# Two-layer MLA / sparse-attention / PEER trunk on one core: layer 1 reordered (indexer blocks first, selection between value blocks, attention two heads at a time inside the key projection, TensorE's order written out), and four query blocks of each PEER loaded early

## The chip, the core and the metric

One core of a Trainium2 chip runs the whole program. The metric is the device time of one execution in microseconds (us). The engines are named as in the profile: PE (matrix multiplication), PEld (PE's weight loads), DVE (vector engine), ACT (scalar engine), POOL (GpSimd), SP (the queue that issues the loads). They run side by side, each through its own list of instructions in order, and wait for each other through semaphores.

## What is computed

256 frames of 1024 channels go through two layers, in fp32 accuracy. Cut to what matters here:

```
layer 0: x = LayerNorm(alpha*x + MLA(x));   x = LayerNorm(alpha*x + PEER(x))
layer 1: x = LayerNorm(alpha*x + DSA(x));   x = LayerNorm(alpha*x + PEER(x))

DSA:  q, k, v (8 heads of 128), q_idx (8 heads of 64), k_idx (64), w_idx (8) = x @ w_in
      q, k, q_idx, k_idx = rope(...)
      idx_score = sum_h w_idx[h] * relu(q_idx[h] . k_idx), masked to chunks of 64 frames
      sel = top_k(idx_score, 64)          # the keys that a frame may look at
      out = softmax(q . k[sel] * 128**-0.5) . v[sel];   out @ w_o
PEER: q = x @ w_q (16 half-queries of 128);  s = q . sub_keys (16 times 128 scores)
      the 16 best expert pairs per head -> gate;  sum over experts of gate * gelu(x . down) * up
```

## The kernel before

**Operands.** Every large product is done in three passes over split operands: a weight block `raw` (128x1024 fp32, 512 KB) is loaded by SP into a ring of 4, ACT copies its high part `hi` (L83, `CAST`), and `lo = raw - hi` is made by DVE (L85), or by POOL for every third block while `ws.share` is 3. The rings of `hi` and `lo` hold 4 blocks each. `Stream.get` hands out block i and queues the `hi` and `lo` of block i+3 and the load of block i+6, so a `CAST` of block i+4 can start only when PE is done with block i. The input, transposed, is held as `xh`, `xl`. `proj` (L221) multiplies one block into a head's 128x256 tile (24 matmuls); `rows` (L238) multiplies the rows of the input by a block 512 columns at a time (12 matmuls for both halves of the frames). All matmuls are issued through `mm` (L213).

**PSUM.** There are 8 banks: four in a ring (`ps`), and four with fixed names (`py(0)` to `py(3)`).

**Layer 1's DSA** (`dsa`, L642). The order of the weight blocks is set by `ws.add`: eight value blocks, four indexer-query blocks (`qi`), the indexer-key block (`ki`, with the 8 columns of w_idx), eight query blocks `q`, eight key blocks (tiles also named `q`), eight blocks of the output projection. The first four value blocks are multiplied while layer 0 still ends. `heads` (L703) does two heads of queries or keys and then `rope`: two partition-swapping copies on ACT (L444, L445), one product on DVE (L448), one on POOL (L449), a sum on DVE (L452). Between the query heads stand `weigh` (L682: w_idx transposed on PE into `wi`) and `select` (L688: 8 small matmuls `il`, relu on ACT, weighted sums on DVE at L696, then 8 rounds of max and replace on DVE, L699 and L700, and the selection mask at L701), for each half of the frames.

**Attention** (`attention`, L454). `scores(h)` makes two score tiles (128 and 256 keys wide): matmul `s`, mask and row maximum on DVE (L470), a small product for the bias (L472), exponential on ACT (L473), reciprocal and scaling on DVE (L475). `output(h)` transposes the probabilities on PE into `pt` (L482 to L484), copies them back on ACT (L486), and multiplies by v into `o`, which is split into `xh`, `xl`. In layer 1 the last two key heads stand between `scores(1)` and the rest; the tile scheduler decides how the remaining PE instructions interleave. Both layers use this function. After it `out_proj` (L500) runs four heads of the output projection, and `finish` (L325) the last four with the residual sum and the LayerNorm, and, as `lead`, the first four query blocks of PEER, multiplied in rows into `qw`.

**PEER** (`peer`, L723). It begins by copying the two `qw` tiles to SBUF (L747), transposing them on PE (`qwT`, L750) and copying them back (L751). Then come the scores against the sub-keys (`ps`) for these four half-queries, the other twelve half-queries (`pq`, `proj` on two blocks each) with their scores in turn, and the search for experts (`choose`, L774, almost all DVE), which runs beside the `down` products (`d`) that follow.

Of the kernel before, what the change touches and what calls it, by code (L numbers as in the profile page):

```python
# [18 lines left out]
P = 128  # L19
# [24 lines left out]
FIRST = 4  # L44
GSCALE = 2.0 ** 14
# [5 lines left out]
class Stream:  # L51
# [5 lines left out]
    def __init__(self, nc, raw, hi, lo):  # L57
        self.nc, self.raw, self.hi, self.lo = nc, raw, hi, lo
        self.blocks, self.ready = [], []
        self.n_loaded = self.n_split = self.n_taken = 0  # L60
        self.tiles = []
        self.share = 0
# [4 lines left out]
    def _load(self, upto):  # L67
        while self.n_loaded <= min(upto, len(self.blocks) - 1):
            src, w = self.blocks[self.n_loaded]
            t = self.raw.tile([P, D], F32, tag="raw", name=f"raw{self.n_loaded}")  # L70
            self.last = self.nc.sync.dma_start(t[:, :w], src).ins
            self.tiles.append(t)
            self.n_loaded += 1

# [72 lines left out]
def tile_trunk(ctx: ExitStack, tc: tile.TileContext, ins, out: bass.AP):  # L147
# [55 lines left out]
    ws.add(ins["dsa_v"])  # L203
    ws.add(ins["dsa_iq"])
    ws.add(ins["dsa_ik"], 576)
    ws.add(ins["dsa_qk"])
# [4 lines left out]

    def mm(o, l, r, start, stop):
        return nc.tensor.matmul(o, l, r, start=start, stop=stop, skip_group_check=True)  # L213

    def mm3(o, lpair, rpair, start, stop):
# [3 lines left out]
        mm(o, ll, rh, False, stop)  # L219

    def proj(o, blk, w=P):  # L221

        h, l = blk
        for c in range(NC):
            s = slice(c * w, (c + 1) * w)
            mm3(o, (h[:, s], l[:, s]), (xh[:, c, :], xl[:, c, :]), c == 0, c == NC - 1)
# [227 lines left out]
    def attention(qk, v, mask, scale, oh, ol, ar, meanwhile):  # L454

        sring = ar.ring(6, T)
# [3 lines left out]
        def scores(h):  # L460
            pr = []
            for t in range(2):
# [3 lines left out]
                for i, (qT, kT) in enumerate(pairs):  # L466
# [12 lines left out]
        def output(h):  # L479
            pr = probs.pop(h)  # L480
            p = py(h % 2, f"pt{h}")
            nc.tensor.transpose(p[:, 0:128], pr[0], ident)  # L482
            nc.tensor.transpose(p[:, 128:256], pr[1][:, 0:128], ident)
            nc.tensor.transpose(p[:, 256:384], pr[1][:, 128:256], ident)  # L484
            pt = tring()
            nc.scalar.copy(pt, p[:, 0:384])  # L486
            o = py(2 + h % 2, f"o{h}")
# [3 lines left out]

        scores(0)
        scores(1)
        meanwhile()
        for h in range(HEADS):
            if 0 < h < HEADS - 1:
                scores(h + 1)
            output(h)
# [505 lines left out]
```

## Time and profile before

| what | value |
|---|---|
| median of 3 runs | 1878.99 us (1876.62 to 1880.26) |
| the profiled execution: its time | 1878.64 us |
| its span in the trace | 1876.7 us |
| granted PE clock, mean over the span | 0.998 |
| PE busy | 1840.9 us, 98% |
| DVE / ACT / POOL busy | 1326.3 us, 71% / 1052.4 us, 56% / 577.9 us, 31% |
| instructions | 33300, of which 12482 matmuls |

The span is what lies between the first and the last instruction in the trace; the execution's time is 1.9 us longer, and the median 0.35 us above that. A matmul's end is modelled: in a row of back-to-back 128x256 matmuls each is shown as 0.28 us long while the next starts 0.12 us after it, so idle time after a matmul is shown 0.16 us too short. DSA lies at about 930 to 1051 us of the span, the start of the two PEERs at 108 and 1062 us.

### The profile page before, as it was taken

What the parts mean: (1) busy time and instruction counts of PE and PEld (TensorE: products, weight loads), DVE (VectorE), ACT (ScalarE), POOL (GpSimd) and SP (SyncE); (2) the same over time, 40 slices, a digit from 0 to 9 for tenths busy, and PEclk for the clock granted to TensorE, in tenths of its full rate; (3) what the DMA queues carried; (4) which work ended last, traced back from release to release, by engine and by line L of the source; (5) the groups of instructions that cost most, each with busy time, mean ns of one, the idle gap of its engine ahead of it and who ended that gap; (6) DMA issues with size and microseconds to landing.
All of it is one profiled execution on the core that took longest, in us unless ns stands there. A gap on an engine that the chain in (4) does not pass through costs nothing. (4 is left out here: it accounts for less than half of the span.)

```text
span 1876.7 us, 33300 instructions
## 1 busy us (share of the span) xinstructions
PE 1840.9 (98%) x12482; PEld 1655.3 (88%) x12482; DVE 1326.3 (71%) x2764; ACT 1052.4 (56%) x1827; POOL 577.9 (31%) x650
## 2 busy tenths in 40 slices
PE   8999999999999999999998999999999999999998
PEld 7889999999998888888797799999999988888886
DVE  5679985788875555555678789957788765555555
ACT  6655455777764444444466445547777654444443
POOL 2001542999930000000032005509999700000000
PEclk9999999999999999999999999999999999999999
DMA  6455555444456555555654555564444465555553
GB/s 227 153 194 179 180 191 172 155 158 158 158 175 228 184 188 191 188 185 189 211 168 148 191 163 180 176 206 155 158 158 152 165 229 186 190 189 185 187 190 113
DMA packets 93762, 335.51 MB, mean 179 GB/s; under 512 B 10400, under 2 KB 11424, under 8 KB 93600
## 3 DMA queue, kind: packets, MB, share of 16 engines
q1 hardware_dynamic: 93312, 332.87, 52.9%
q8 instruction: 97, 1.59, 0.3%
q14 instruction: 65, 0.53, 0.1%
q10 hardware_dynamic: 288, 0.52, 0.1%
HBM read 329.16 MB, written 4.19 MB: 178 GB/s over the span
## 5 line engine op out<-in xcount | busy, mean ns | idle before, releaser
L85 DVE TENSOR_TENSOR lo<-raw,hi 128x1024 fp32r<-128x1024 f32 x587 | 725.6, 1238 | 365.7 <-ACT hi L83 364.6
L83 ACT CAST hi<-raw 128x1024 fp32r<-128x1024 f32 x592 | 618.8, 1046 | 591.7 <-PE d L213 259.5
L213 PE MATMUL d<-xh,hi 128*128 128x256 f32 x2048 | 579.4, 283 | 0.0
L213 PE MATMUL d<-xh,lo 128*128 128x256 f32 x2048 | 572.8, 280 | 0.9 <-DVE lo L85 0.9
L213 PE MATMUL d<-xl,hi 128*128 128x256 f32 x2048 | 572.9, 280 | 0.0
L847 POOL TENSOR_SCALAR VU<-iota,i2t 128x128 f16<-128x128 f16 x512 | 430.8, 859 | 112.1 <-DVE i2t L836 100.5
L213 PEld LDWEIGHTS d<-xh,lo 128*128 128x128 f32 x2048 | 384.5, 188 | 1.3 <-DVE lo L85 1.3
L213 PEld LDWEIGHTS d<-xh,hi 128*128 128x128 f32 x2048 | 384.7, 188 | 0.0
L213 PEld LDWEIGHTS d<-xl,hi 128*128 128x128 f32 x2048 | 384.1, 188 | 0.0
L213 PE MATMUL y<-lo,xh 128*128 128x512 f32 x1088 | 345.4, 394 | 0.0
L213 PE MATMUL y<-hi,xh 128*128 128x512 f32 x1088 | 345.0, 394 | 0.0
L213 PE MATMUL y<-hi,xl 128*128 128x512 f32 x1088 | 344.7, 394 | 0.0
L293 POOL TENSOR_TENSOR st<-st,mhalf 128x1 f32<-128x1 f32 x8 | 4.4, 554 | 855.2 <-DVE st L291 855.2
L213 PEld LDWEIGHTS y<-hi,xl 128*128 128x128 f32 x1088 | 203.5, 187 | 50.4
L213 PEld LDWEIGHTS y<-lo,xh 128*128 128x128 f32 x1088 | 203.4, 187 | 50.5 <-DVE lo L85 0.6
L213 PEld LDWEIGHTS y<-hi,xh 128*128 128x128 f32 x1088 | 203.4, 187 | 49.9
L848 DVE TENSOR_SCALAR VU<-iota,i1t,gt 128x128 f16<-128x128 f16 x512 | 139.2, 349 | 58.4 <-PE G L213 33.3
L849 ACT ACTIVATE U<-VU,gr 128x128 f16<-128x128 f16 x512 | 170.1, 399 | 1.2 <-DVE gr L832 0.7
L903 ACT CAST xh<-arena 128x512 fp32r<-128x512 f32 x128 | 79.4, 621 | 154.5 <-PE y L213 149.2
L904 DVE TENSOR_TENSOR xl<-arena,xh 128x512 fp32r<-128x512 f32 x128 | 88.1, 691 | 82.0 <-ACT xh L903 82.0
L802 POOL TENSOR_TENSOR arena<-arena 128x800 f32<-128x800 f16 x32 | 79.0, 2488 | 41.0 <-DVE arena L800 40.1
L213 PE MATMUL G<-VU 128*128 128x128 f16 x512 | 71.4, 221 | 6.9 <-DVE VU L848 4.1
(224 smaller groups left out, 1819.8 us busy)
## 6 DMA issues: line engine op xcount, KB each, us to landing
raw<-in_down SPq DMA_DIRECT2D x256, 512.0 KB, 3.3
raw<-in_up SPq DMA_DIRECT2D x256, 512.0 KB, 4.2
raw<-in_peer_q SPq DMA_DIRECT2D x32, 512.0 KB, 4.6
raw<-in_dsa_qk SPq DMA_DIRECT2D x16, 512.0 KB, 3.3
raw<-in_mla_w_o SPq DMA_DIRECT2D x8, 512.0 KB, 5.2
raw<-in_dsa_v SPq DMA_DIRECT2D x8, 512.0 KB, 3.5
raw<-in_dsa_w_o SPq DMA_DIRECT2D x8, 512.0 KB, 4.5
raw<-in_mla_qk SPq DMA_DIRECT2D x7, 512.0 KB, 4.7
```

The source lines that it names most:

```text
L83: nc.scalar.copy(hi, raw)
L85: eng.tensor_tensor(lo, raw, hi.bitcast(F32), op=ALU.subtract)
L213: return nc.tensor.matmul(o, l, r, start=start, stop=stop, skip_group_check=True)
L293: nc.gpsimd.tensor_tensor(st[:, 5:6], st[:, 4:5], mhalf, op=ALU.pow)
L802: nc.gpsimd.tensor_tensor(o.rearrange("p k c -> p c k"), same, cell[t][:, h, :, None].to_broadcast([P, CELLS, TOPK]), op=ALU.mult)
L847: nc.gpsimd.tensor_scalar(V, iota16, i2t[:, t : t + 1], None, op0=ALU.is_equal)
L848: nc.vector.tensor_scalar(U, iota16, i1t[:, t : t + 1], gt[:, t : t + 1], op0=ALU.is_equal, op1=ALU.mult)
L849: nc.scalar.mul(L, U, gr[:, t : t + 1])
L903: nc.scalar.copy(hh, a)
L904: nc.vector.tensor_tensor(al, a, hh.bitcast(F32), op=ALU.subtract)
```

## The change

Six things are done in one edit.

1. *Blocks of layer 1.* Order now: value blocks 0 to 3, `qi`, `ki`, value blocks 4 to 7, queries, keys, output projection. `weigh` stands behind value block 4; `select` became a generator, and `pick(n)` issues the next n of its `il` steps after each half of value blocks 5 to 7 and in the query projection.
2. *TensorE's order.* From value block 4 to the end of attention every PE instruction is tied behind the one emitted before it (`pe`, `chained`), so PE's list is the order of the code.
3. *Attention of layer 1.* Heads are done in pairs inside the key projection: scores of 0, 1 after two key pairs, and so on; heads 4 to 7 alternate with the first four heads of the output projection (`project`), and their `pt` and `o` use the ring `ps`. In layer 0 the scores run two heads ahead of the output. In both layers the product at L472 is dropped: the reduction scales, takes the minimum of the negated scores, and the exponential has scale -1.
4. *`lo` on POOL* only during the query projection, not during the key projection.
5. *PEER's start, both layers.* The transposes of `qw` are placed behind the first of the two blocks of `pq4`; then the scores of the first four half-queries, and the rest.
6. *Early loads, both layers.* When the output projection starts, PEER's query blocks 4 to 7 are loaded into a free part of the arena instead of into the ring `raw`. The loads of the residual `x` and of the LayerNorm's gain and bias are issued before the key projection.

```
+    def ahead(self, behind, places):
+        for i, t in enumerate(places, self.n_taken + behind):
+            assert i >= self.n_loaded and self.blocks[i][1] == D
+            self.last = self.nc.sync.dma_start(t, self.blocks[i][0]).ins
+            self.early[i] = t
...
-    ws.add(ins["dsa_v"])
+    ws.add(ins["dsa_v"][0:FIRST])
     ws.add(ins["dsa_iq"])
     ws.add(ins["dsa_ik"], 576)
+    ws.add(ins["dsa_v"][FIRST:NC])
     ws.add(ins["dsa_qk"])
...
+    def pe(emit):
+        with ExitStack() as order:
+            if chain["on"] and chain["last"] is not None:
+                order.enter_context(tc.issue_after(chain["last"]))
+            ins = emit()
+        chain["last"] = ins.ins
+        return ins
...
-        sring = ar.ring(6, T)
+        sring = ar.ring(2 * ahead + 2, T)
...
-                nc.vector.tensor_tensor_reduce(out=s, in0=p[:, :nk], in1=mask[t], scale=1.0, scalar=GONE,
-                                               op0=ALU.add, op1=ALU.max, accum_out=m[:, 0:1])
-                nc.vector.tensor_scalar(m[:, 1:2], m[:, 0:1], scale[t], -1.0, op0=ALU.mult, op1=ALU.mult)
-                nc.scalar.activation(s, s, AF.Exp, bias=m[:, 1:2], scale=scale[t], accum_out=m[:, 2:3])
+                nc.vector.tensor_tensor_reduce(out=s, in0=p[:, :nk], in1=mask[t], scale=scale[t], scalar=-GONE,
+                                               op0=ALU.add, op1=ALU.min, accum_out=m[:, 0:1])
+                nc.scalar.activation(s, s, AF.Exp, bias=m[:, 0:1], scale=-1.0, accum_out=m[:, 2:3])
...
+            p = ps(f"pt{h}") if late and h >= 4 else py(h % 2, f"pt{h}")
...
+            o = ps(f"o{h}") if late and h >= 4 else py(2 + h % 2, f"o{h}")
...
+        meanwhile(2)
+        pair(scores, 0)
+        meanwhile(4)
+        pair(scores, 2)
+        pair(turned, 0)
+        meanwhile(6)
+        pair(output, 0)
+        pair(turned, 2)
+        pair(scores, 4)
+        pair(output, 2)
+        pair(scores, 6)
+        for h in range(4, 8, 2):
+            late(h - 4, 0)
+            pair(turned, h)
+            late(h - 4, 1)
+            pair(output, h)
+            late(h - 3, 0)
+            late(h - 3, 1)
+
+    def project(oh, ol, h, t):
+        if h == t == 0:
+            with tc.issue_after(ws.last):
+                ws.ahead(HEADS + FIRST, [arena[:, EARLY + i * D : EARLY + (i + 1) * D] for i in range(4)])
+            begun["y4"] = [[py(2 * i + n, f"y{i}{n}") for n in range(2)] for i in range(2)]
+        if t == 0:
+            begun["w"] = ws.get()
+        rows(begun["y4"], (oh[:, h, :], ol[:, h, :]), begun["w"], h == 0, False, (t,))
...
+        chained(True)
+        v4 = begun.pop("v4")
+        for c in range(FIRST, NC):
+            for t in range(2):
+                rows(v4, (xh[:, c, :], xl[:, c, :]), blk := ws.get() if t == 0 else blk, False, c == NC - 1, (t,))
+                if c > FIRST:
+                    pick(2)
+            if c == FIRST:
+                weigh()
+                pick(1)
...
         ws.share = DSA_POOL
         for h in range(0, HEADS, 2):
-            heads(qT, h)
-            (weigh, lambda: select(0), lambda: select(1), lambda: None)[h // 2]()
-        for h in range(0, HEADS - 2, 2):
-            heads(kT, h)
+            heads(qT, h, lambda: pick(2))
+            pick(3)
+        pick(9)
+        ws.share = 0
...
+        queries(4)
+        scores(0)
+        queries(6)
+        scores(1)
+        for g4 in range(2, 4):
+            queries(4 * g4)
+            queries(4 * g4 + 2)
+            scores(g4)
```

The lists of the engines show three places at which instructions stand otherwise. In them a number behind `hi`, `q`, `o` or `pq` tells one tile from the next. The rows begin with the line of the kernel that issues the instruction: L95, L475, L476, L742, L743, L747, L748, L97, L479, L483, L260, L261, L518, L845 and L852 of the changed kernel are L83, L444, L445, L675, L676, L680, L681, L85, L448, L452, L229, L230, L486, L747 and L751 of the one before.

**First place: behind the indexer's key.** ACT's list of before, from the copies of `ki`:

```order
L83 CAST hi_10438<-raw_10336 128x1024
L675 COPY arena<-ki 32x256
L676 COPY arena<-ki 32x256
L83 CAST hi_10468<-raw_10366 128x1024
L681 ACTIVATE arena<-ki 8x256
L680 COPY arena<-arena 64x256
```

and of the changed kernel:

```order
L95 CAST hi_10341<-raw_10240 128x1024
L742 COPY arena<-ki 32x256
L743 COPY arena<-ki 32x256
L95 CAST hi_10363<-raw_10270 128x1024
L748 ACTIVATE arena<-ki 8x256
L747 COPY arena<-arena 64x256
```

In both a `CAST` stands ahead of the `ACTIVATE` that makes w_idx. Before, the next reader, `wi` on PE, comes 56 matmuls of the projections later. In the changed kernel `hi_10363` is in the ring the successor of `hi_10236`, which is value block 4, and PE's list has `wi` directly behind the last matmul of that block:

```order
L240 MATMUL v_10073<-lo_10237,xh 128x512
L240 MATMUL v_10072<-hi_10236,xl 128x512
L240 MATMUL v_10073<-hi_10236,xl 128x512
L243 MATMUL wi<-ident,arena 128x8 x2
L240 MATMUL v_10070<-hi_10266,xh 128x512
```

The `il` that follow are between the value blocks now; before, PE met `wi` inside the query projection.

**Second place: the end of the key projection.** PE's list of before, where `q6` is the tile of key heads 6 and 7, `sht` the scores of head h and half t, `pt` the transposed probabilities and `o` the output:

```order
L213 MATMUL q6_11037<-xl_91,hi323_10936 128x256
L213 MATMUL q6_11037<-xh_90,lo323_10937 128x256
L213 MATMUL s20_11113<-arena_98 128x128
L213 MATMUL s21_11121<-arena_98 128x256
L482 MATMUL pt0_11103<-ident_84,arena_98 128x128
...
L213 MATMUL s41_11173<-arena_98 128x256
L213 MATMUL s50_11191<-arena_98 128x128
L213 MATMUL o0_11108<-arena_98 128x256
L213 MATMUL o0_11108<-arena_98 128x128
L213 MATMUL s51_11199<-arena_98 128x256
L213 MATMUL o1_11134<-arena_98 128x256
```

and of the changed kernel:

```order
L240 MATMUL q6_11051<-xl_91,hi323_10948 128x256
L240 MATMUL q6_11051<-xh_90,lo323_10949 128x256
L240 MATMUL o0_11117<-arena_98 128x256
L240 MATMUL o0_11117<-arena_98 128x128
L240 MATMUL o1_11122<-arena_98 128x256
L240 MATMUL o1_11122<-arena_98 128x128
L243 MATMUL pt2_11127<-ident_84,arena_98 128x128 x3
```

Scores and transposes stood behind `q6`; now the outputs of heads 0 and 1 stand there. `o1` uses `py(3)`, the bank of `q6`. ACT's list of the changed kernel at this place:

```order
L95 CAST hi326_11082<-raw326_10952 128x1024
L95 CAST hi327_11211<-raw327_10982 128x1024
L475 COPY arena_98<-q6_11051 64x512
L476 COPY arena_98<-q6_11051 64x512
L260 CAST xh_90<-o0_11117 128x256
L260 CAST xh_90<-o1_11122 128x256
L518 COPY arena_98<-pt2_11127 128x384
```

and DVE's:

```order
L97 TENSOR_TENSOR lo326_11083<-raw326_10952,hi326_11082 128x1024
L97 TENSOR_TENSOR lo327_11212<-raw327_10982,hi327_11211 128x1024
L479 TENSOR_TENSOR arena_98<-q6_11051,arena_98 128x512
L261 TENSOR_TENSOR xl_91<-o0_11117,xh_90 128x256
L483 TENSOR_TENSOR arena_98<-arena_98 128x512
```

`hi327` is in the ring the successor of `hi323`, the block that the last matmul of `q6` reads. It stands ahead of the two copies that read `q6`, and its `lo327` ahead of the product that reads `q6`.

**Third place: the start of PEER in layer 1.** PE's and ACT's lists of before:

```order
L213 MATMUL qw1_11460<-lo335_11450,xh_90 128x512 x2
L213 MATMUL qw1_11460<-hi335_11449,xl_91 128x512 x2
L750 MATMUL qwT0_11537<-ident_84,arena_98 128x128 x4
L750 MATMUL qwT1_11544<-ident_84,arena_98 128x128 x4
L213 MATMUL pq10_11562<-xh_90,hi336_11563 128x256
```

```order
L83 CAST hi336_11563<-raw336_11498 128x1024
L747 COPY arena_98<-qw0_11459 128x512
L83 CAST hi337_11567<-raw337_11501 128x1024
L747 COPY arena_98<-qw1_11460 128x512
L751 COPY arena_98<-qwT0_11537 128x4x128
L83 CAST hi338_11571<-raw338_11517 128x1024
L751 COPY arena_98<-qwT1_11544 128x4x128
```

and of the changed kernel:

```order
L240 MATMUL pq4_11498<-xl_91,hi336_11499 128x256
L240 MATMUL pq4_11498<-xh_90,lo336_11500 128x256
L851 MATMUL qwT0_11545<-ident_84,arena_98 128x128 x4
L851 MATMUL qwT1_11551<-ident_84,arena_98 128x128 x4
L240 MATMUL pq4_11498<-xh_90,hi337_11503 128x256
```

```order
L845 COPY arena_98<-qw0_11427 128x512
L845 COPY arena_98<-qw1_11428 128x512
L95 CAST hi339_11511<-arena_98 128x1024
L95 CAST hi340_11557<-raw340_11515 128x1024
L852 COPY arena_98<-qwT0_11545 128x4x128
L852 COPY arena_98<-qwT1_11551 128x4x128
```

The transposes moved behind the 24 matmuls of the first block of `pq4`; the two copies of `qw` are no longer parted by a `CAST` of a block that comes through the ring `raw`.

## Rows read from the trace of the kernel before

**Rows 1.** The page: the span, the busy time of each engine, and the line of PE's granted clock in 40 equal slices, and the group of all `lo` on DVE (idle time behind the busy time and the mean).

```profile
span 1876.7 us, 33300 instructions
...
PE 1840.9 (98%) x12482; PEld 1655.3 (88%) x12482; DVE 1326.3 (71%) x2764; ACT 1052.4 (56%) x1827; POOL 577.9 (31%) x650
...
PEclk9999999999999999999999999999999999999999
...
L85 DVE TENSOR_TENSOR lo<-raw,hi 128x1024 fp32r<-128x1024 f32 x587 | 725.6, 1238 | 365.7 <-ACT hi L83 364.6
```

**Rows 2.** What PE waited for over the whole span: its tile and line, the releaser, us in total, times, longest.

```profile
PE qwT L750 <- ACT arena L747: 4.0, 4, 1.6
PE s L213 <- DVE arena L452: 2.8, 1, 2.8
...
PE s L213 <- DVE m L470: 1.0, 2, 0.7
...
PE d L213 <- DVE lo L85: 0.9, 2, 0.6
```

**Rows 3.** Three stretches of layer 1: us, then for each engine its busy time and instructions, PE's granted clock, the share of the DMA engines and GB/s.

```profile
930.40:1003.00 72.60, 69.78 (x540) 65.25 (x538) 55.23 (x95) 44.19 (x68) 24.79 (x13) 1.00 0.49 165
1003.00:1007.00 4.00, 4.00 (x17) 3.69 (x18) 3.96 (x10) 2.44 (x3) 1.77 (x1) 0.57 0.63 200
...
1012.00:1028.00 16.00, 13.56 (x77) 10.52 (x76) 14.21 (x74) 13.12 (x42) 2.16 (x1) 1.00 0.43 159
```

**Rows 4.** PE in order of time at the first scores: start, us, the instruction, and in brackets the idle time before it with its releaser.

```profile
999.87 0.28 PE L213 MATMUL q<-xh,lo 128*128 128x256 f32 x1
1002.98 2.45 PE L213 MATMUL s<-arena 128*128 128x128 f32 x8 [2.83 <-DVE arena L452]
```

**Rows 5.** DVE in order of time, at three places of the query and key projections.

```profile
960.14 2.51 DVE L679 TENSOR_TENSOR arena<-arena 64x256 f32<-64x256 f32 x1
...
998.60 3.39 DVE L85 TENSOR_TENSOR lo<-raw,hi 128x1024 fp32r<-128x1024 f32 x1
...
1002.25 0.67 DVE L452 TENSOR_TENSOR arena<-arena 128x512 f32<-128x512 f32 x1
...
1007.25 0.29 DVE L701 TENSOR_SCALAR arena<-arena 128x256 f32<-128x256 f32 x1
```

**Rows 6.** POOL in order of time at the same places.

```profile
959.74 2.63 POOL L85 TENSOR_TENSOR lo<-raw,hi 128x1024 fp32r<-128x1024 f32 x1 [1.98 <-ACT hi L83]
...
998.53 2.38 POOL L85 TENSOR_TENSOR lo<-raw,hi 128x1024 fp32r<-128x1024 f32 x1 [0.24 <-ACT hi L83]
...
1014.63 2.16 POOL L449 TENSOR_TENSOR arena<-arena 128x512 f32<-128x512 f32 x1 [8.59 <-ACT arena L445]
```

**Rows 7.** PE in order of time in the attention behind the key projection: the five instructions that waited.

```profile
1014.05 1.23 PE L213 MATMUL s<-arena 128*128 128x128 f32 x4 [0.27 <-DVE m L470]
1015.99 0.49 PE L213 MATMUL s<-arena 128*128 128x128 f32 x2 [0.71 <-DVE m L470]
...
1020.04 0.30 PE L482 MATMUL pt<-ident,arena 128*128 128x128 f32 x1 [0.36 <-DVE arena L475]
...
1023.49 0.92 PE L213 MATMUL o<-arena 128*128 128x256 f32 x4 [0.19 <-ACT arena L486]
...
1025.78 0.92 PE L213 MATMUL o<-arena 128*128 128x256 f32 x4 [0.76 <-ACT arena L486]
```

**Rows 8.** PE in order of time at the transposes of `qw`, layer 0 and layer 1.

```profile
112.82 0.66 PE L750 MATMUL qwT<-ident,arena 128*128 128x128 f32 x4 [1.60 <-ACT arena L747]
114.25 0.66 PE L750 MATMUL qwT<-ident,arena 128*128 128x128 f32 x4 [0.78 <-ACT arena L747]
...
1065.83 0.66 PE L750 MATMUL qwT<-ident,arena 128*128 128x128 f32 x4 [0.57 <-ACT arena L747]
1067.52 0.66 PE L750 MATMUL qwT<-ident,arena 128*128 128x128 f32 x4 [1.03 <-ACT arena L747]
```

**Rows 9.** ACT in order of time, behind the indexer's key and at the start of PEER in layer 1.

```profile
958.62 1.05 ACT L83 CAST hi<-raw 128x1024 fp32r<-128x1024 f32 x1 [0.38 <-PE q L213]
959.81 0.37 ACT L681 ACTIVATE arena<-ki 8x256 f32<-8x256 f32 x1
...
1064.24 1.05 ACT L83 CAST hi<-raw 128x1024 fp32r<-128x1024 f32 x1 [6.28 <-DMA raw<-in_peer_q]
1065.20 0.58 ACT L747 COPY arena<-qw 128x512 f32<-128x512 f32 x1
1065.93 1.05 ACT L83 CAST hi<-raw 128x1024 fp32r<-128x1024 f32 x1 [0.16 <-DMA raw<-in_peer_q]
```

**Rows 10.** PE in order of time around a group of `il`.

```profile
967.20 0.28 PE L213 MATMUL q<-xl,hi 128*128 128x256 f32 x1
967.32 0.28 PE L213 MATMUL q<-xh,lo 128*128 128x256 f32 x1
967.52 0.72 PE L213 MATMUL il<-arena 64*128 64x128 f32 x8
968.17 0.39 PE L213 MATMUL q<-xh,hi 128*128 128x256 f32 x1
```

**Rows 11.** The experts' search in both layers: first stretches as in rows 3 (the queries and the beginning of the search, then the rest of it, for each layer).

```profile
118.60:158.90 40.30, 40.30 (x348) 40.30 (x347) 33.47 (x145) 18.95 (x25) 0.00 (x0) 1.00 0.54 177
158.90:264.20 105.30, 104.73 (x891) 104.53 (x889) 105.12 (x367) 54.51 (x63) 49.87 (x48) 1.00 0.52 173
```

More of the change, by code (lines that the diff above doesn't have):

```diff
@@ L44 @@
 FIRST = 4
+EARLY = 11264
 GSCALE = 2.0 ** 14
@@ L61, in __init__ @@
         self.tiles = []
+        self.early = {}
         self.share = 0
@@ L452, in rope, with attention @@
             nc.vector.tensor_tensor(place, t1[r], xs[r], op=ALU.add)
-    def attention(qk, v, mask, scale, oh, ol, ar, meanwhile):
-        sring = ar.ring(6, T)
+    def attention(qk, v, mask, scale, oh, ol, ar, ahead, meanwhile, late=None):
+        sring = ar.ring(2 * ahead + 2, T)
         tring = ar.ring(2, 384)
@@ L490, in output, with pair, out_proj @@
             split_ps(oh[:, h, :], ol[:, h, :], o[:, 0:256])
[L492 to L498, printed above, removed]
-    def out_proj(oh, ol, g, b, x, spare):
-        y4 = [[py(2 * t + n, f"y{t}{n}") for n in range(2)] for t in range(2)]
-        for h in range(HEADS - STAGGER):
-            rows(y4, (oh[:, h, :], ol[:, h, :]), ws.get(), h == 0, False)
+        if not late:
+            for h in range(HEADS + ahead):
+                if h < HEADS:
+                    meanwhile(h)
+                    scores(h)
+                if h >= ahead:
+                    turned(h - ahead)
+                    output(h - ahead)
+            return
+        def pair(f, h):
+            f(h)
+            f(h + 1)
+        meanwhile(2)
[24 more added lines that the diff above has]
+        rows(begun["y4"], (oh[:, h, :], ol[:, h, :]), begun["w"], h == 0, False, (t,))
+    def out_proj(oh, ol, g, b, x, spare, start):
+        for h in range(start, HEADS - STAGGER):
+            for t in range(2):
+                project(oh, ol, h, t)
+        y4 = begun.pop("y4")
         finish(y4, lambda h: (oh[:, h, :], ol[:, h, :]), HEADS, g, b, x, spare, lead_queries)
@@ L637, in qk @@
             return [(qn[:, h, :], kn[:, h, :]), (qr[:, h // 2, h % 2, :], kr)]
-        attention(qk, v, mask, [rq[:, t : t + 1] for t in range(2)], oh, ol, ar, values)
-        out_proj(oh, ol, g, b, x, r2)
+        attention(qk, v, mask, [rq[:, t : t + 1] for t in range(2)], oh, ol, ar, 2,
+                  lambda h: values() if h == 2 else None)
+        out_proj(oh, ol, g, b, x, r2, 0)
     def dsa():
@@ L658, in dsa @@
         m8 = ar.take(2, 8)
-        v4 = begun.pop("v4")
-        for c in range(FIRST, NC):
-            rows(v4, (xh[:, c, :], xl[:, c, :]), ws.get(), False, c == NC - 1)
-        for t in range(2):
-            for n in range(2):
-                nc.scalar.copy(v[:, t, n * 512 : (n + 1) * 512], v4[t][n])
         for h in range(0, HEADS // 2, 2):
@@ L690, in select @@
             for h in range(HEADS):
+                yield
                 r = slice((h % 2) * 64, (h % 2) * 64 + 64)
@@ L701, in select, with heads @@
             nc.vector.tensor_scalar(sel[t], acc[t], GONE / 2, NEG, op0=ALU.is_gt, op1=ALU.mult)
-        def heads(dst, h):
+        def heads(dst, h, between=lambda: None):
             p = py(h // 2, f"q{h}")
```

88 lines of the change are left out of this document (60 added, 28 removed).

## The prediction

> **What bounds the kernel now.** I read the page first: PE is busy 1840.9 of 1876.7 us and its granted clock shows no tenth below 9 in any slice [rows 1]. So TensorE is the bound; the change alters neither number nor kind of its matmuls, and can gain only what PE stands idle or runs at the lower clock, 36 us in all. The list of what PE waits for is next: the largest waits that the diff touches are the transposes of `qw` behind their copies on ACT (4.0 us, 4 times), one wait of the first scores for a rope sum on DVE (2.8), and small ones in attention [rows 2]. Then I cut layer 1 into stretches. [...]
>
> Why the first scores waited is read on DVE and POOL. PE's last key matmul starts at 999.87, the scores at 1002.98 [rows 4]; they need the sum at L452, which DVE begins at 1002.25, because a `lo` ahead of it took 3.39 us [rows 5], while POOL made another `lo` from 998.53 for 2.38 us [rows 6]. All 587 `lo` on DVE take 1.24 us on average [rows 1]. The same picture stands at 960.14: a DVE sum of 64x256 takes 2.51 us [rows 5], and its neighbour of the same shape 0.41, while POOL's `lo` runs from 959.74 to 962.37 [rows 6]. DVE's selection, too, ran beside the key projection, to 1007.25 [rows 5].
>
> **Removed.** (a) The stand of the first scores: 3.11 us from start to start instead of the 0.12 of neighbouring matmuls [rows 4, 10], 3.0 us. After the change the selection is spread over the value blocks and the query projection, no POOL `lo` falls into the key projection, and the first scores come only after two further key blocks; nothing is queued ahead of the rope sum but the `lo` of one or two blocks. (b) The lower clock behind it: 4.00 x (1 - 0.57) = 1.7 us [rows 3]. (c) The gaps in attention: 2.44 us shown [rows 3], plus 0.16 us for each of the five main ones, since a matmul's end is drawn that much late [rows 7, 10]: 3.2 us. In the new list the scores have a whole key pair (48 matmuls, 5.6 us at 0.117) or an output-projection half between them and their readers. Together 7.9 us.
>
> **Added in attention's stage.** (d) `wi` now stands directly behind value block 4, and what makes its input stands on ACT behind a `CAST` that cannot start before that block's last matmul. PE waits for the `CAST` (1.05 us) and the `ACTIVATE` (0.37) [rows 9], and two hand-overs between engines, for which I take 0.1 each (the switch into `il`, 0.20 from start to start instead of 0.12, is the nearest row [rows 10]): 1.65 us, at least 1.4. Queued behind `wi` on PE is everything. Its cover before was 56 matmuls. (e) At the end of the key projection `o0` and `o1` follow `q6`, and `o1` takes `q6`'s bank. DVE reads that bank in third place: the `CAST` of a block that waits for `q6`'s last matmul (1.05) [rows 9], its `lo` (1.24) [rows 1], then the product, of the size of the sum at L452 (0.67) [rows 5], and two hand-overs: 3.15 us. `o0`'s two matmuls cover some 0.65: 2.5 us stand. ACT's two copies of `q6` (0.58 each is my estimate, the price of a 512-wide copy [rows 9]) end earlier, 2.4 us after `q6`; if DVE should come before its `lo`, PE would stand 1.7. So 1.7 to 2.5; I take 2.5, since DVE's list is in that order. (f) The `il` come in eight groups instead of five. One group takes 0.85 us between its neighbours' starts [rows 10], a third of it switching: 0.3 for each of three, 0.9 us (0.3 to 1.2). (g) Switches between outputs, transposes and output-projection halves in the written order: 0.5 (0 to 1). (h) Scores that come just behind a key pair wait for its rope. By DVE's walk through the key projection (two `lo` of 1.24, a product and a sum of 0.67, so 3.8 us per pair of 5.6, behind copies on ACT and a product on POOL) the sum is ready up to 0.8 us ahead or late; with the gain and bias loads now ahead of a key block, later still: 0.8 (0 to 2.4). Together 6.35 us, so the stage as a whole gives 7.9 - 6.35 = 1.55 us.
>
> **Peer's start.** The transposes now stand behind 24 matmuls (2.8 us at 0.117). ACT's two copies of `qw`, 1.2 us, are done by then, with no `CAST` of a late block between them: in layer 1 that block's `CAST` had waited 6.28 us for its load, and the next one parted the copies [rows 9]. Layer 0 gains 1.60 + 0.78 + 2 x 0.16, less 0.2 for the switch in and out of `pq`: 2.5. Layer 1: 0.57 + 1.03 + 0.32 - 0.2 = 1.7 [rows 8]. Together 4.2 us, and this needs `hi` and `lo` of the first block ready when `qw` ends, which the early loads give: they move bytes that were loaded anyway to a time when the DMA engines are busy 0.43 of the time [rows 3]. SP issues them in front of output-projection blocks, whose loads have over 10 us of spare by the order; if not, up to 2 us is lost.
>
> **At nothing:** the dropped product at L472 (the gaps it was in are counted under c), and layer 0's attention, where the order differs in a few places: 0, within 0.4 either way.
>
> **Sum.** 1.55 + 4.2 = 5.75. The profiled execution took 1878.64 us, so 1872.9; the median is 0.35 above it: 1873.2 us, 0.31% faster. About 0.2%, 3.8 us, can be told from no change here.
>
> **Rivals.**
> 1. *The clock falls in stand (e).* Before, 2.83 us of idle were followed by a granted 0.57 [rows 3, 4]; 1.60 and 0.78 us shortly after each other [rows 8] left no such mark. Stand (e) is shown as 2.35 us, between the two. If the clock falls, another 1.7 us goes: 1874.9, still faster by 0.22%, at the edge. Chance 0.17.
> 2. *DVE is the bound in the search, and takes the 4.2 us back.* From 158.9 to 264.2 DVE is busy 105.12 of 105.30 us [rows 11], and PE waits for a `lo` at its end [rows 2]. If DVE's search starts no earlier than before, PE only waits there instead. Against it: in the stretch ahead DVE is busy 33.47 of 40.30 us [rows 11], so 6.8 us of idle lie between the earlier start and the dense part, and DVE's work is the same. If it holds for both layers 4.2 of 5.75 is lost: 1877.4, no change. Chance 0.1.
> 3. *The key projection's rope sums come late at every pair.* DVE takes two `lo` more in this projection than before and POOL's product (2.16 us when beside DVE work [rows 6]) ends last. Three stands, each 0.8 longer than (h) has it, 2.4, and one stretch at the lower clock, 1.7: 1877.3, no change. Chance 0.08.
> 4. *Slower: POOL stops DVE through the whole stage.* Three `lo` and six rope products on POOL (2.4 and 2.2 us [rows 6]) now lie beside the selection's DVE work, which stood partly in the idle time of PE's clean stretch. If each of the nine holds DVE for 2 us (the `lo` of 3.39 instead of 1.24 [rows 1, 5]), DVE comes 18 us late in a stage where it has, by 55.23 busy of 72.60 [rows 3], some 17 us of idle; beyond that every us lands on PE. It decides when DVE is late by more than that: with half of the idle unusable, 18 - 8.5 = 9.5 us are lost, the gain of 5.75 against it: 1878.99 - 5.75 + 9.5 = 1882.7, slower by 0.2%; more idle unusable gives more. Against it: there were five POOL `lo` in the stage before, three now. Chance 0.05. [...]
> 5. *The change doesn't do what it says in attention*: the pairs are tied to one written order, where PE could before take whatever came first, and (c) returns as other gaps of the same sum, DVE's maxima and ACT's exponentials being no shorter. Then the gain is 5.75 - 3.2 = 2.55: 1876.4, no change. Chance 0.1.
>
> **How the numbers follow.** Forecast (1872.9 by the sum, 1873.2 as a median) 0.5; rivals 0.17, 0.1, 0.08, 0.05 and 0.1. The forecast's own range follows from the bounds: (e) at 1.7, (f), (g) and (h) at their low ends give 0.8 + 0.6 + 0.5 + 0.8 = 2.7 us more gain, 1870.5; the high ends take 0.3 + 0.5 + 1.6 = 2.4, 1875.6. Below, an upside that I cannot price but do not exclude (gaps in layer 0) takes it to 1869.5; above, rivals 2, 3 and 5 reach 1877.4 and are taken in. Faster by over 0.2% (below 1875.2): forecast 0.46 of its 0.5, rival 1 0.12, and a share of the others: 0.66. Slower: 0.06. Same: 0.28.
>
> **What would show it.** In the trace after: no wait of the first scores over 1 us and no stretch at half clock in 990 to 1010; `qwT` without a wait in both layers; one wait of `wi` of 1.4 to 1.9 us for ACT about 945 us; one of `o1` of 1.7 to 2.5 us (shown 0.2 less) for DVE or ACT near the key projection's end; il groups between the value blocks; DVE done with L701 before the first scores. Wrong if `s` waits at the key pairs, if PE's wait for `lo` at the end of the searches grows by 2 us, or if DVE ends a POOL-held instruction just ahead of a PE wait.

## The result, and the profile after

The changed kernel takes 1867.79 us (median of 4, 1866.95 to 1869.07) where the one before takes 1879.62: ratio 0.9939, 95% interval 0.9925 to 0.9953; a second comparison gave 0.9942 (0.9929 to 0.9956). The forecast was 1873.2 (1869.5 to 1877.4): right in direction, but the gain was 11.8 us (10.6 in the second comparison) instead of 5.75, and the time lies below the range.

The page of the changed kernel, the span and the busy times, and then from PE's waits over the span those that matter here, with their line, releaser, total, number and longest, as [rows 1, 2] of before:

```profile
span 1867.2 us, 33267 instructions
...
PE 1836.0 (98%) x12482; PEld 1652.4 (88%) x12482; DVE 1323.4 (71%) x2734; ACT 1051.5 (56%) x1827; POOL 572.8 (31%) x648
```

```profile
PE o L240 <- DVE arena L479: 2.4, 1, 2.4
...
PE wi L243 <- ACT arena L748: 1.6, 1, 1.6
...
PE s L240 <- DVE arena L483: 0.9, 1, 0.9
...
PE d L240 <- DVE lo L97: 0.7, 2, 0.4
```

Three things left the list: `qwT` (4.0 us), the first scores' 2.8, the gaps in attention. Two came, where forecast: `wi` 1.6 and `o1` 2.4. In order of time, PE at these two places, at the first scores (992.85), which no longer wait, and at the second pair of scores (1000.86), which waits for the sum of the key pair just ahead of it:

```profile
944.03 0.28 PE L243 MATMUL wi<-ident,arena 8*128 8x8 f32 x2 [1.56 <-ACT arena L748]
...
992.85 1.50 PE L240 MATMUL s<-arena 128*128 128x128 f32 x8
...
1000.86 0.71 PE L240 MATMUL s<-arena 128*128 128x128 f32 x3 [0.85 <-DVE arena L483]
...
1008.58 0.81 PE L240 MATMUL o<-arena 128*128 128x256 f32 x4
1011.83 0.89 PE L240 MATMUL o<-arena 128*128 128x256 f32 x4 [2.43 <-DVE arena L479]
```

ACT at `wi` and at `o1`, and DVE at `o1`:

```profile
942.50 1.04 ACT L95 CAST hi<-raw 128x1024 fp32r<-128x1024 f32 x1 [0.46 <-PE v L240]
943.60 0.37 ACT L748 ACTIVATE arena<-ki 8x256 f32<-8x256 f32 x1
...
1008.71 1.04 ACT L95 CAST hi<-raw 128x1024 fp32r<-128x1024 f32 x1 [1.54 <-issue]
1009.78 0.58 ACT L475 COPY arena<-q 64x512 f32<-64x512 f32 x1
1010.38 0.58 ACT L476 COPY arena<-q 64x512 f32<-64x512 f32 x1
```

```profile
1009.79 1.22 DVE L97 TENSOR_TENSOR lo<-raw,hi 128x1024 fp32r<-128x1024 f32 x1 [0.83 <-ACT hi L95]
1010.99 0.69 DVE L479 TENSOR_TENSOR arena<-q,arena 128x512 f32<-128x512 f32 x1
1011.60 0.41 DVE L261 TENSOR_TENSOR xl<-o,xh 128x256 fp32r<-128x256 f32 x1
```

The chain of `wi` is that of step (d): the `CAST` starts when its block's last matmul ends (942.50), and the `ACTIVATE` follows. That of `o1` begins as step (e) has it, with the `CAST` at 1008.71. Then the `lo` on DVE and the two copies of `q6` on ACT run side by side and end together (1011.01 and 1010.96); the product at L479 starts at 1010.99 and ends at 1011.68, and `o1` starts at 1011.83. Which of the two the product waits for can't be told here; the run with the `CAST` of `hi327` moved tells it.

The transposes at the start of PEER, which waited in [rows 8], in layer 1, with ACT's copies of `qw`:

```profile
1060.61 0.28 PE L240 MATMUL pq<-xh,lo 128*128 128x256 f32 x1
1060.73 1.03 PE L851 MATMUL qwT<-ident,arena 128*128 128x128 f32 x8
```

```profile
1057.71 1.06 ACT L845 COPY arena<-qw 128x512 f32<-128x512 f32 x2
```

They follow `pq` at the usual spacing (0.12 us). Where the time went, by the stretches of the trace (us between the first PE instructions of the named tiles; before three times, since two more profiles were taken, see below; "stage" is layer 1 from its first `xt` to its first `qw`):

| execution | input, to `krope` | to `y` (layer 0 attention) | PEER start, `xt` to `d` | stage | PEER start, `qw` to `d` |
|---|---|---|---|---|---|
| before, first profile | 25.3 | 47.5 | 58.2 | 136.0 | 56.1 |
| before, second | 24.0 | 47.5 | 57.9 | 136.0 | 56.9 |
| before, third | 24.1 | 47.4 | 59.3 | 136.0 | 57.8 |
| changed, first | 24.7 | 46.7 | 55.4 | 133.8 | 54.1 |
| changed, second | 24.5 | 46.8 | 55.4 | 133.9 | 54.1 |

The stretches of layer 0's output projection (23.9) and up products (358.4) are equal to a tenth in all. With parts 5 and 6 in, the two starts of PEER took 55.35 to 55.37 and 54.09 to 54.10 us in each of ten profiles.

### The profile page after: what moved, and what is told of

It reads as the page before. It is cut to its first block, busy times and chain, and to the rows that moved or that the text cites. A ratio compares the mean times of both kernels' runs of the same rounds, so it can differ in the third digit from the quotient of the medians.

```text
span 1867.2 us, 33267 instructions
## 1 busy us (share of the span) xinstructions
PE 1836.0 (98%) x12482; PEld 1652.4 (88%) x12482; DVE 1323.4 (71%) x2734; ACT 1051.5 (56%) x1827; POOL 572.8 (31%) x648
## 5 line engine op out<-in xcount | busy, mean ns | idle before, releaser
L97 DVE TENSOR_TENSOR lo<-raw,hi 128x1024 fp32r<-128x1024 f32 x581 | 715.8, 1233 | 357.4 <-ACT hi L95 356.5
L95 ACT CAST hi<-raw 128x1024 fp32r<-128x1024 f32 x584 | 610.5, 1046 | 585.5 <-PE d L240 258.6
L1017 ACT CAST xh<-arena 128x512 fp32r<-128x512 f32 x128 | 79.4, 621 | 154.5 <-PE y L240 149.2
```

The source lines that it names most:

```text
L95: nc.scalar.copy(hi, raw)
L97: eng.tensor_tensor(lo, raw, hi.bitcast(F32), op=ALU.subtract)
L1017: nc.scalar.copy(hh, a)
```

## The experiments

Ratios are to the kernel before in the same comparison.

**The changed kernel again.** No edit.

> The changed kernel once more, unaltered, with a second profile. In the first pair of profiles layer 1's attention stage is 2.2 us shorter, the starts of the two PEERs 2.7 and 2.0, layer 0's attention 0.7, and 1.9 us more lie in stretches that the diff does not touch (layer 0's input projection 0.9, the down products and the gate products 1.0). Theory A (the steps of the forecast are right, and what is missing is the clock and chance): again 10 to 12 us faster than before; in the second profile the untouched stretches differ from those of the first by about 0.5 to 1 us, and the lower clock behind the wait of wi may be gone (1.7 us less). Theory B (something that the forecast lacks works in the untouched stretches): they have the same times as in the first profile within 0.2 us.

1868.61 us, 0.9942 (0.9929 to 0.9956). The clock now stayed up behind `wi`, and fell behind `o1`:

```profile
942.00:951.00 9.00, 7.43 (x29) 4.93 (x29) 4.59 (x10) 3.70 (x9) 0.00 (x0) 0.81 0.34 117
```

```profile
1009.00:1016.00 7.00, 5.78 (x28) 5.42 (x29) 4.57 (x19) 3.88 (x12) 1.27 (x1) 0.76 0.42 150
```

(first profile, then the second; PE's clock is the third number from the end: 0.81 over 9 us, 0.76 over 7). Each has one fall ahead of the last microseconds of the span, in different places, and the stage is 133.8 and 133.9. The untouched stretches came out as in the first profile within 0.2 us, as theory B had it; but where they differ from before most, in the input stretch, it was before's first profile that did not repeat (25.3, then 24.0 and 24.1).

**PEER's start alone**, in the kernel before:

```
+        with tc.issue_after(ws.last):
+            ws.ahead(HEADS + FIRST, [arena[:, EARLY + i * D : EARLY + (i + 1) * D] for i in range(4)])
         for h in range(HEADS - STAGGER):
...
+            if n == FIRST:
+                with tc.issue_after(first.ins):
+                    turn()
...
+        queries(4)
+        scores(0)
```

> The kernel before with parts 5 and 6 alone: the transposes of qw behind the first block of pq4, and the four early loads in each layer. Theory A: 4.2 to 4.8 us faster (ratio 0.9975), all of it at the two starts of PEER: no wait of qwT; nothing in the down products. Theory B (the early loads relieve the loads later): 6 us or more, seen in the stretches behind PEER's queries. The sum's rival (DVE's search takes it back): under 1 us, with a longer wait of d for lo at the end of the searches.

1870.3 us, 0.9951 (0.9938 to 0.9965): 9 us, twice the forecast. Its profile has 55.4 and 54.1 us in the two starts, the changed kernel's own, and the stage of before, 136.0; the down products behind the starts are no shorter (154.5 and 154.3 us, before 154.5 and 154.2). `qwT` has left the list of PE's waits. So the gain lies where theory A has it, but is as large as theory B has it.

**The rest alone:** the changed kernel with before's start of PEER and no early loads.

> The changed kernel without parts 5 and 6: PEER starts as before, no early loads; layer 1's stage and the attention of both layers as changed. Theory A: 1.55 us by the sum; 2.2 + 0.7 = 2.9 by the first pair of profiles, and up to 1.7 more in executions in which the clock does not fall behind wi: 3 to 4.6 us faster (ratio 0.9976 to 0.9984). Theory B: 6 us or more.

1875.47 us, 0.998 (0.9971 to 0.9989), 3.7 us, as theory A has it. Against the changed kernel in the same comparison (1868.61) parts 5 and 6 are worth 6.9 us. The starts of PEER took 59.6 and 58.5 us here, 1.4 and 2.4 more than in the first profile of before, with the same instructions:

```profile
110.00:117.00 7.00, 5.25 (x31) 5.02 (x32) 4.90 (x4) 5.21 (x8) 0.00 (x0) 0.76 0.76 242
1062.00:1070.00 8.00, 5.62 (x35) 5.38 (x35) 4.90 (x4) 5.83 (x8) 0.00 (x0) 0.79 0.70 245
```

Behind the stands of `qwT` (where PE stood still for its input) the clock was down (0.76 and 0.79 in the mean of these stretches).

**Layer 0's attention alone**, in the kernel before.

> The kernel before with only layer 0's attention as changed (scores two heads ahead, the small product dropped). By the forecast 0 within 0.4; by the first pair of profiles 0.7 us faster (the stretch from the first scores to the output projection 18.9 to 18.2 us). Theory B: 2 us or more.

1879.26 us, 0.9997 (0.9988 to 1.0006): not to be told from no change. In the profile the stretch is 46.8 instead of 47.5, as in every kernel with it, and the clock fell behind layer 0's `qwT` (0.50 from 114 to 116 us; 58.2 became 59.8).

**The kernel before, profiled twice more.**

> The kernel before, unaltered, for a second profile. The prediction priced the stands of qwT (1.60 + 0.78 and 0.57 + 1.03 us) from one execution in which the clock did not fall behind them; in two other kernels with the same start of PEER it fell behind them in three of four places. Theory A (the fall behind these stands is a matter of chance): in this or the next profile the clock falls at 112 or 1066 us, and the start of that PEER is 1 to 2 us longer (58.1 to about 59.8 us from the first xt to the first d). The input projection, 25.3 us in the first profile and 23.9 to 24.7 in all others, comes out near 24. Theory B: both as in the first profile.

> A third profile of the kernel before; the same expectations as for the second.

In the second the input stretch is 24.0, and `qwT` of layer 1 waits 1.61 and 0.78 us instead of 0.57 and 1.03; the clock stays up, as in the first. In the third it fell behind both stands of `qwT`; first the two stretches in the first profile, then in the third:

```profile
111.00:117.00 6.00, 3.62 (x29) 3.17 (x29) 3.68 (x3) 5.77 (x8) 0.00 (x0) 1.00 0.74 242
1064.00:1071.00 7.00, 5.40 (x41) 4.59 (x39) 4.31 (x4) 5.93 (x8) 0.00 (x0) 1.00 0.81 276
```

```profile
111.00:117.00 6.00, 5.00 (x29) 4.76 (x30) 4.62 (x4) 4.47 (x7) 0.00 (x0) 0.72 0.72 229
1066.00:1073.00 7.00, 5.85 (x36) 5.62 (x37) 4.77 (x4) 4.62 (x7) 0.00 (x0) 0.76 0.73 229
```

The stands of layer 0 in the second profile and this stretch in it, then the stands in the third:

```profile
111.22 0.66 PE L750 MATMUL qwT<-ident,arena 128*128 128x128 f32 x4 [1.28 <-ACT arena L747]
112.65 0.66 PE L750 MATMUL qwT<-ident,arena 128*128 128x128 f32 x4 [0.77 <-ACT arena L747]
...
111.00:117.00 6.00, 5.01 (x42) 4.77 (x43) 4.64 (x5) 5.11 (x9) 0.00 (x0) 1.00 0.69 229
```

```profile
111.22 0.66 PE L750 MATMUL qwT<-ident,arena 128*128 128x128 f32 x4 [1.31 <-ACT arena L747]
112.66 1.12 PE L750 MATMUL qwT<-ident,arena 128*128 128x128 f32 x4 [0.78 <-ACT arena L747]
```

Theory A holds: in layer 0 the same stands of 1.3 and 0.8 us are followed by the lower clock in the third execution and not in the second. In layer 1 it fell behind 0.99 and 0.78 us in the third, and not behind the longer 1.61 and 0.78 in the second. Of ten such places (five executions with this start of PEER) five show the fall, and the start is then 59.3 to 59.8 us instead of 58 in layer 0, 57.8 to 58.5 instead of 56.4 in layer 1.

**The early loads taken out** of the changed kernel.

> The changed kernel without the early loads: PEER's query blocks 4 to 7 come through the ring raw, the transposes stay behind the first block of pq4. If the early loads carry part of the gain: PE waits at pq4 for hi and lo of that block, which before came 1.05 + 1.24 us after a load that landed at 1064.2, so 1.3 to 1.8 us in layer 1 and about the same in layer 0; 3 us slower than the changed kernel, more where the clock falls behind it. If the place of the transposes alone makes the gain: within 0.5 us of the changed kernel.

1873.24 us, 0.9962 (0.9948 to 0.9975). PE's waits:

```profile
PE pq L240 <- ACT hi L95: 2.4, 2, 1.5
...
PE pq L240 <- DVE lo L97: 1.5, 2, 0.8
```

3.9 us in two layers, and a fall of the clock behind each (0.50 from 112 to 114 and from 1064 to 1066 us; the starts 59.1 and 58.5). In this execution the moved transposes gain 0.6 us without the loads, against the starts of the run without both (59.6 and 58.5): the stand goes from `qwT` to `pq`. But it is the slowest of the six executions (1875.99), and by the ratios, from two comparisons, the kernel is 0.0018 or 3.4 us ahead of that run (0.9962, and 0.998 there; the intervals overlap a little). What the place of the transposes gives by itself is not settled.

**`wi` half a block later** (its `il` move with it).

```
-                if c > FIRST:
-                    pick(2)
-            if c == FIRST:
-                weigh()
-                pick(1)
+                if c == FIRST + 1 and t == 0:
+                    weigh()
+                    pick(1)
+                elif c > FIRST:
+                    pick(2)
```

> The changed kernel with weigh behind the first half of value block 5 instead of directly behind block 4. If the wait of wi (1.6 us) is the cause of a loss, it is gone (under 0.3 us) and the kernel is 1.3 to 1.6 us faster than the changed one, about 1867; the clock can then fall only behind o1. If the clock falls wherever the stage offers a stand, the mean clock stays 0.998 in most executions; if the falls came with the wait of wi, it rises to 0.999 in more of them.

1870.01 us, 0.9949: not faster. The wait of `wi` went to 0.2, and the first scores' came back:

```profile
PE s L240 <- DVE arena L483: 2.7, 1, 2.7
PE o L240 <- DVE arena L479: 2.4, 1, 2.4
...
PE wi L243 <- ACT arena L748: 0.2, 1, 0.2
```

with the clock down for some 7 us behind it (0.57 in the mean of 993 to 1001 us); the stage took 136.4. With two `il` fewer between the value blocks the selection ends on DVE at 988.0 instead of 986.0 us, and the rope sum that the first scores need starts at 993.5 instead of 992.0.

**ACT's `CAST` of `hi327` behind the copies of `pt2` and `pt3`** (`copied` is the copy of `pt3`).

```
+        begun["cast"] = begun["copied"]
...
+            with tc.issue_after(begun["cast"]):
+                begun["w"] = ws.get()
```

> The changed kernel with the CAST of the first output-projection block but three (hi327) placed behind the copies of pt2 and pt3 in ACT's list, so that it no longer stands ahead of the two copies that read q6. By the forecast's chain (CAST 1.05, lo 1.24, product 0.7) o1 then waits for two copies of 0.58 and a hand-over, 1.4 us behind q6, of which o0 covers 0.65: its wait falls from 2.4 to 0.7 to 1.0 us, 1.4 to 1.7 us in the end. If something else held the bank, the wait stays above 2 us. At under 1 us no fall of the clock is expected behind it.

1867.57 us, 0.9936 (0.9922 to 0.995). The wait of `o1` fell to 1.4, not to 0.7 to 1.0, the stage from 133.8 to 132.9. ACT and DVE behind `q6`:

```profile
1008.48 0.58 ACT L475 COPY arena<-q 64x512 f32<-64x512 f32 x1 [1.68 <-PE q L240]
1009.09 0.58 ACT L476 COPY arena<-q 64x512 f32<-64x512 f32 x1
```

```profile
1009.70 0.69 DVE L479 TENSOR_TENSOR arena<-q,arena 128x512 f32<-128x512 f32 x1 [1.10 <-ACT arena L476]
```

No `lo` is in the way any more, and DVE stands idle for 1.10 us: the product waits for ACT's second copy. So the bank is held by two copies and the product, and the wait fell by the `CAST` alone (1.04).

**Both, and `o0`, `o1` in the ring `ps`.**

> The two edits together, and o0 and o1 in the ring ps, so that o1 waits for nothing of q6. No wait over 1 us in layer 1's stage but that of the first scores (0.9). If the steps add, 4 us (1.6 + 2.4) less than the changed kernel, and another 1 to 1.7 for the clock, which has no stand left to fall behind: 1863 to 1865, mean clock 0.999 in nearly all executions. If the stands only move (to s50 or o2, behind ACT's copies of pt2), 1 us of it comes back.

1868.25 us, 0.9942: no wait of `wi` or `o1`, but the first scores at 2.7 again, as with `wi` later alone; this time the clock stayed up behind them (1.00 from 993 to 1000 us). The stage took 132.1.

**`wi`'s input ahead on ACT instead**, with the `il` left where they are; then also the ring for `o0`, `o1` (`turned_w` is the `ACTIVATE` that makes w_idx).

```
+            if c == FIRST:
+                with tc.issue_after(turned_w):
+                    blk = ws.get()
```

> The changed kernel with the copies and the product of ki placed ahead of two CASTs on ACT, so that wi finds its input (the il stay where they are), and with hi327's CAST behind the copies of pt2 and pt3. Theory A (the waits of wi and o1 are what the forecast says they are): no wait of wi, o1 1.4 us, no fall of the clock behind them: 2.6 us for the two waits and about 1 us for the clock under the changed kernel, 1864 to 1865 where that takes 1868.5. Theory B (DVE's selection sets the time of the first scores, so that PE, earlier by 1.6 us, waits there instead): the first scores wait 1.5 to 2.7 us, with a fall of the clock, and the kernel is within 1 us of the changed one.

> The same with o0 and o1 in the ring ps, so that o1 need not wait for the bank of q6. As for the run before, and 1 us less if the wait of o1 (1.4) goes without coming back at s50 or o2; no difference if it comes back.

1863.38 us, 0.9922 (0.9908 to 0.9935), and 1862.65, 0.9916 (0.9903 to 0.993). The stage takes 130.0 and 129.0, the clock falls nowhere before the last 5 us of the span. The first scores wait in neither. Waits in the second, of the second pair of scores and of `pt`:

```profile
PE s L240 <- DVE arena L483: 0.8, 1, 0.8
...
PE pt L243 <- DVE arena L507: 0.7, 1, 0.7
```

So the two new waits (1.6 and 2.4) and the fall behind one of them had cost 133.8 - 129.0 = 4.8 us, with the wait of `pt` (0.7) that came back already taken off.

**The middle of attention not in pairs**, on that kernel: `o0`, `pt2`, `s4`, `o1`, `pt3`, `s5`, `o2`, `s6`, `o3`, `s7`.

> The kernel of the last run (wi_cast_ring) with the middle of the attention not in pairs: o0, pt2, s4, o1, pt3, s5, o2, s6, o3, s7. In the kernel before, attention's s, pt and o matmuls took 5.2 us more than their back-to-back spacing, 3.1 of it in the five named waits; in the last kernel 0.5. Theory A (turning from one kind of matmul to another costs, and pairs halve the turns): the excess rises by 0.1 to 0.2 us for each of some 6 more turns, 0.6 to 1.2 us, with no new wait over 0.3 us. Theory B (only the waits differ, and their cover is the order of the heads): the excess without waits stays at 0.5 within 0.3, or the loss is in new waits that the list of waits names.

1863.13 us, 0.9908 (0.9891 to 0.9925). The excess of s, pt and o over their back-to-back spacing, added up from their starts, is 0.53 us, against 0.46 in pairs; theory B. The stage, 128.7, is the shortest of all.

**`lo` on POOL in the key projection too** (part 4 undone).

> The changed kernel with part 4 undone: POOL makes every third lo in the key projection and attention too (7 instead of 3). If a lo on POOL holds DVE (2.4 to 3.4 us instead of 1.24, as beside the five of the kernel before), the rope sums come late again: the first scores wait 2 to 3 us instead of 0.9, the clock falls behind them, 2 to 4 us slower than the changed kernel. If DVE gains more by the work that it loses (four lo of 1.24), no slower, and o1, whose product stood behind such a lo on DVE, waits 1.2 us less.

1872.01 us, 0.9957 (0.994 to 0.9973), the stage 138.0. PE's waits there:

```profile
PE s L240 <- DVE arena L483: 3.1, 1, 3.1
PE o L240 <- DVE arena L479: 2.3, 1, 2.3
PE wi L243 <- ACT arena L748: 1.6, 1, 1.6
```

and the groups of `lo` on POOL and on DVE between 955 and 1030 us:

```profile
L97 POOL TENSOR_TENSOR lo<-raw,hi 128x1024 fp32r<-128x1024 f32 x6 | 17.1, 2848 | 37.8 <-DVE arena L767 20.8 <-ACT hi L95 14.0 <-DVE arena L483 2.9
```

```profile
L97 DVE TENSOR_TENSOR lo<-raw,hi 128x1024 fp32r<-128x1024 f32 x13 | 17.1, 1318 | 7.4 <-ACT hi L95 7.4
```

With six `lo` of 2.85 us on POOL instead of three, the wait of 3.1 and the clock's fall at 994 us (0.50 from 996 to 998) are back. One line of the diff thus carries 4 us of the stage; without it the stage is 2 us longer than before. DVE made 13 `lo` there instead of 18, at 1.32 us on average instead of 1.24, and was late all the same. POOL and DVE ahead of the first scores show why:

```profile
986.84 3.33 POOL L97 TENSOR_TENSOR lo<-raw,hi 128x1024 fp32r<-128x1024 f32 x1 [2.87 <-DVE arena L483]
990.13 1.29 POOL L480 TENSOR_TENSOR arena<-arena 128x512 f32<-128x512 f32 x1
```

```profile
992.40 1.23 DVE L97 TENSOR_TENSOR lo<-raw,hi 128x1024 fp32r<-128x1024 f32 x1 [3.69 <-ACT hi L95]
993.54 0.69 DVE L483 TENSOR_TENSOR arena<-arena 128x512 f32<-128x512 f32 x1
```

The rope product (L480) stands behind the `lo` in POOL's list, and the sum (L483) behind the `lo` of a later block in DVE's, whose `CAST` comes only when PE has done the last key matmul ahead of the scores. DVE was not held here; it stood idle for 3.69 us. The wait of `o1` gained almost nothing (2.3).

## Why the prediction was wrong

The step that failed most is the price of the start of PEER: 4.2 us in the sum, 6.6 in the traces, 6.9 to 8.9 in the times of the runs with and without it. The other misses are smaller.

- **(a), (d), (h)** came as priced: 3.0 us gone; `wi` 1.6 (1.65); the scores 0.9 (0.8).
- **(e)** has the right size, `o1` 2.4 shown and 2.6 from start to start (2.5), but one wrong link, and so part of it is luck: DVE's product could not have come ahead of ACT's two copies of `q6`, which take as long (2 x 0.58) as the `lo` that the sum has in their place (1.22).
- **(f)** was too high by the mechanism that it names. From the matmul ahead of each group to the one behind it, less one usual spacing, the `il` cost 4.6 us before and 5.5 in the first profile, 0.9 more as forecast; but the first group ran at the lower clock there (0.50 from 946 to 948 us; 1.06 us instead of 0.53). In the second profile, where it did not, they cost 4.9, 0.3 more.
- **(b)** failed as a term of its own, not in the sum. In the kernel with PEER's start alone the clock does not fall behind the first scores (1.00 from 998 to 1010 us, where they wait 2.8), and the stage is 136.0 as before: PE is ahead and waits longer in attention instead (`pt` 1.4 us instead of [rows 7]'s 0.36). DVE set that end; (b) and (c) had to be one term of 4.9.
- **(g)** failed: 0.5 us for switching in attention. Its matmuls exceeded their spacing by 5.2 us before, 3.1 of it in the five waits of (c); after the change nothing but `o1`'s wait is left. So some 2 us of short gaps, a part of which is the first scores at the lower clock, went too and no 0.5 came. The order singly instead of in pairs had the same excess, so it is not the number of turns. What made the short gaps of before stays open; most stand just behind a wait.
- **The start of PEER**, 4.2 us, was priced from one execution in which the clock did not fall behind the stands, and the text took that for a rule ("left no such mark"). In layer 1 that execution also had the shortest stands of the five (1.60 us together, in the others 1.68 to 2.49). Over five executions with the old start it takes 59.0 and 57.1 us, after 55.4 and 54.1: 6.6 us. In the places without a fall the gain is 2.65 and 2.3, 5 us and 0.8 above the sum; the falls in half of the places make the other 1.6.
- **Rival 1**, the clock behind (e), came true in one of two profiles; in the other it fell behind `wi`, which no case had. The first profile of before and both of the changed kernel show one fall each, but the executions at large differ: in the comparison with 21 executions of before, the mean clock was 0.999 in three (mean 1877.0 us), 0.998 in five (1878.6), 0.997 in ten (1879.5) and 0.996 in three (1880.9). The fall of [rows 3], 4.00 us at 0.57 (0.50 from 1003.60 to 1006.90), takes 1.7 us or 0.0009 of the span, so each step is about one fall; this is an estimate, since the clock is also down in the last 3 to 5.5 us of the spans (0.50 in the last 2.8 us of before's first profile and in the last 3.9 of the changed kernel's). The changed kernel showed 0.998 or 0.999 in nine of nine. Nor is a long stand always followed by a fall: behind first scores that waited 2.8 and 2.7 us the clock stayed at 1.00 in the run with PEER's start alone and in the one with three edits, and fell to 0.50 in all three profiles of before (behind 2.83 us in the first).
- **Layer 0's attention**, 0 within 0.4, gave 0.7 in every trace; its own comparison can't tell it.
- **Rival 2** did not happen: PE's wait for `lo` at the end of the searches went from 0.9 to 0.7. **Rivals 3 and 4** did not either, but the runs with `wi` later and with POOL's `lo` kept show how near: the stage is then 2.6 and 4.2 us longer. The POOL `lo` of part 4, which the sum had inside (a) with no price of its own, decides the sign in this stage, by the one profile without it. What was late there stood in line behind a `lo`; it was not held by one, as rival 4 would have it.
- **What remains:** 6.6 + 2.2 + 0.7 = 9.5 of the 10.6 to 11.8 us. Both profiled executions of the changed kernel were the slowest of their comparison (1869.07 and 1869.30 us): from the three profiled executions of before (1879.3 in the mean) to these two it is 10.1 us. The rest is spread over stretches that the change doesn't touch, and over executions; it is not settled. Parts 1 to 3 of the change were not tried singly, so the 2.2 us of the stage are not shared out among them.

## What to carry to other kernels

Here the clock fell (to 0.50 to 0.55 over 2 us) behind five of ten places where PE stood for 1.6 to 2.5 us, and the start of PEER was then 1.3 to 2.1 us longer. Such a stand is to be priced with the fall that may follow, as an expectation over executions and not from the one that was profiled; of three profiles of the kernel before only the third shows it. Moving a waiting instruction later was of no use here, because what came behind it then came too late: where the input could be made earlier on ACT, the wait went and stayed away (1863.38 us with the `CAST` moved too); where the reader was moved, the wait came back elsewhere (1870.01 us). Work given to POOL cost time here though DVE had less to do (six `lo` on POOL between 955 and 1030 us instead of three, 13 on DVE instead of 18; the stage took 138.0 us instead of 133.8): in the lists of POOL and DVE, look at what stands ahead of the instruction that PE waits for.

## What the runs showed of the hardware

The same 256-column matmuls run at two spacings at a granted clock of 1.00. In the query and key projections they are 0.1178 us apart up to the last `il` (980.76 us in the first profile of before, 965.23 in that of the changed kernel), then 0.1133, in each of the sixteen profiles; this lasts until about the first scores in fourteen of them, and only to 983 us, eleven before the first scores, in the two with `wi` moved later. In the down products some 45 us ran at 0.1133 in six profiles, three in each layer (152.5 us for the stretch instead of 154.2; in layer 1 the run without parts 5 and 6, the one with `wi` later and the one with the `CAST` later), in kernels whose down products are the same as in the others; so 1.7 us between two executions can come from there. Two stretches of 20 us of these products in the run without parts 5 and 6, with PE's busy time and its matmuls first and the granted clock third from the end:

```profile
1180.00:1200.00 20.00, 20.00 (x173) 20.00 (x172) 0.00 (x0) 2.13 (x4) 1.00 0.48 161
1225.00:1245.00 20.00, 20.00 (x179) 20.00 (x178) 0.00 (x0) 2.36 (x4) 1.00 0.67 222
```

173 matmuls in the first, 179 in the second. That had not been expected, and its cause stays open.
